# Sigmoid gates of a hybrid attention layer by seven block products instead of eight, on one Trainium2 core

## The chip, the core and the metric

The kernel runs on one core of one Trainium2 chip, as one launch. TensorE (PE) multiplies matrices into PSUM, VectorE (DVE), ScalarE (ACT) and GpSimd (POOL) work element by element, and SyncE (SP) issues every DMA of this kernel in one queue. The metric is the device time of one execution in microseconds (us); lower is better.

## The reference

One layer of an encoder, batch 1, 1024 tokens, width 1024, all in float32 (cut to what matters):

```python
h = rms_norm(x, g_norm1) * (1.0 + sc1) + sh1
qa, ka, va, qb, kb, vb, gates = split(h @ w_in)
o_a = neighbourhood_attention(norm(qa), norm(ka), va, rpb)        # 8 heads of 64
o_b = mixture_of_dilated_windows(rot(qb), rot(kb), vb)            # 3 x 4 heads of 64
gate_a, gate_b = split(sigmoid(gates + b_gate), 2)                # 1024 columns each
merged = gate_a * (o_a @ w_proj_a) + gate_b * (o_b @ w_proj_b)
x = x + gt1 * (merged @ w_o)
h2 = rms_norm(x, g_norm2) * (1.0 + sc2) + sh2
a, up = split(h2 @ w_ffn_in)                                      # 2816 columns each
x = x + gt2 * ((silu(a) * up) @ w_ffn_out)
```

The change concerns `gates = h @ w_g`, a product of 1024 × 1024 by 1024 × 2048.

## The kernel before

Every float32 matrix product is done as three passes: each operand is split into a rounded part `hi` and a rest `lo`, and the products hi·hi, hi·lo and lo·hi are summed in PSUM (`PASS`). So a product over one tile of 128 input rows is three matmuls. A weight comes as `wload` (a DMA into a `raw` tile of 128×512, six such tiles) and is split by `wsplit` (L108, L109): ScalarE copies it to `whi`, and POOL or VectorE subtracts to `wlo`.

The program is a sequence of stages. Up to about 60 us it makes h, transposed and split, in two tiles `hT` (128 × 8 × 1024 each, hi and lo). Then comes a loop over turns n = 6 to 91 (60 to 628 us), one turn after the other: projections of ten units of attention heads (L293), and with them scores (L442), score maxima on VectorE (L456), transposes (L468) and products with v (L483) of items that are spread over three turns; each turn issues the scores of one item, the transposes of the item of the turn before, and the products of the one before that. A turn of the dilated heads is about 6.15 us long. The last turns, n = 80 to 90, have no projection any more, and half products of the gates fill them (`gate_pre`, L602): 24 matmuls each, with 128 gate columns as weights and 512 tokens as moving data. Two such half products share one weight. Their sums wait in DRAM (`sig_d`).

After the loop come, each starting where TensorE's queue reaches it: the gate stage (`gates`, L580 by `mm_set`), which makes the other 21 half products for i = 2 to 7 (i counts blocks of 128 columns in each of the two gates); the merge (again L580, and L877 to L881), the output projection (L1027), the first FFN matrix (L1091) and the second (L1247).

Both FFN matrices are already done with seven block products in place of eight (Winograd's form of Strassen's scheme, one level): the tokens are two blocks, the inner dimension is two blocks, and a pair of outputs is two blocks. The weight blocks w11, w12 and w22 are used plain, and four combinations x1 to x4 are made from differences; the token blocks are mixed in the same manner (`t_columns`). For the second FFN matrix the weight combinations were made by `w2_combos` (L901 to L908) during the gate stage: four loads of 256 KB, two subtractions each on POOL and VectorE, four stores to `w2_d`, eleven times. `w1_combos` does the like for two blocks of the first FFN matrix.

What sets the order: TensorE's instructions stand in program order, by hand. On the other engines a scheduler orders what the code issues. Each engine then works its queue strictly in order; an instruction that has to wait holds all behind it. SyncE waits in the same way before it issues a DMA.

The tiles that matter: `raw` (6), `whi`/`wlo` (10 each), `l` (22, the landing tiles of `w2_combos`, on the right side of SBUF, beside the ten `sg` tiles of the gates), and the attention's own pool on the right side, which is released after the last turn.

Of the kernel before, what the change touches and what calls it, by code (L numbers as in the profile page):

```python
# [27 lines left out]
LATE = (3, 4, 5, 6, 7)  # L28
# [4 lines left out]
NLAND = 22  # L33
W2C = {0: (0,), 1: (1,), 2: (2, 3), 3: (4,), 4: (5,), 5: (6, 7), 6: (8,), 7: (9,), 8: (10,)}
# [9 lines left out]
def hybrid_layer(ctx: ExitStack, tc: tile.TileContext, x, colp, wada1, wada2, bada2, wqkv, wg, wpa, wpb,  # L44
# [16 lines left out]
    sig_d = tc.dram_tile([4, 2, 128, S], F32, name="sig_d")  # L61
# [522 lines left out]
    NPRE = 11  # L584

    def gate_w(i, br):
        if (i, br) not in gw:
            gw[i, br] = [wslot(wg[i, :, 8 * br + 4 * j:8 * br + 4 * j + 4, :], 512) for j in range(2)]

    def gate_pre(n):  # L590

        i, br, hf = n // 4, (n // 2) % 2, n % 2
        hs = slice(hf * 512, hf * 512 + 512)
        st = {}

        def chunk(k):
            if k == 0:
                gate_w(i, br)
                st["p"] = bank("d")
            j, kk = divmod(k, 4)  # L600
            for q, (a, b) in enumerate(PASS):
                nc.tensor.matmul(st["p"], gw[i, br][j][a][:, kk * 128:(kk + 1) * 128], hT[b][:, k, hs],  # L602
                                 start=(k == 0 and q == 0), stop=(k == 7 and q == 2))
            if k == 7:
                if hf == 0:
                    gsig[i, br] = big("gsig")
                dst = gsig[i, br][:, hs]
                nc.scalar.activation(dst, st["p"], AF.Identity, bias=bg_c[:, 8 * br + i:8 * br + i + 1])
                nc.sync.dma_start(sig_d[i, br][:, hs], dst)

        return [lambda k=k: chunk(k) for k in range(8)]

    gw, gsig = {}, {}
# [145 lines left out]
    for n in range(6, 92):  # L759
# [6 lines left out]
        elif n - 80 < NPRE:  # L766
            chunks = gate_pre(n - 80)
        else:
            chunks = []
# [57 lines left out]
    for br in range(2):  # L827
        gate_w(3, br)
    ap_.release()

    sgp = pool("sig", "right")
    sig = {}

    def sig_tile(i, br):
        z = sgp.tile(wide, F32, tag="sg", bufs=10, name="sg")
        for hf in range(2):
            sig.setdefault((i, br, hf), z[:, hf * 512:hf * 512 + 512])

    for i in LATE:
        for br in range(2):  # L840
            sig_tile(i, br)
    sig[2, 1, 1] = sgp.tile([128, 512], F32, name="s2")
    lnd = pool("land", "right")

    def gates(i, br):
        gate_w(i, br)
        for hf in range(2):
            hs = slice(hf * 512, hf * 512 + 512)
            if i * 4 + br * 2 + hf < NPRE:
                continue  # L850
            pb = bank("ds"[br])
            for j in range(2):
                mm_set(pb, gw[i, br][j], hT, 4 * j, 4, 8, 4 * j, hs)
            nc.scalar.activation(sig[i, br, hf], pb, AF.Sigmoid, bias=bg_c[:, 8 * br + i:8 * br + i + 1])

    def sig_load(i, br, hf):
        if i * 4 + br * 2 + hf < NPRE:
            hs = slice(hf * 512, hf * 512 + 512)
            nc.sync.dma_start(sig[i, br, hf], sig_d[i, br][:, hs])
            nc.scalar.activation(sig[i, br, hf], sig[i, br, hf], AF.Sigmoid)  # L860
# [7 lines left out]
    def merge(i):  # L868
        merge_w(i)
        wa, wb = mw[i]  # L870
        for hf in range(2):
            hs = slice(hf * 512, hf * 512 + 512)
            ppa, ppb = bank("tv"[hf]), bank("ds"[hf])
            mm_set(ppa, wa, oT, 0, 4, 4, 0, hs)
            mm_set(ppb, wb, oT, 4, 2, 2, 0, hs)
# [7 lines left out]
    def o_split():  # L883
        for pr in (4, 5, 0, 1, 2, 3):
            for hf in range(2):
# [519 lines left out]
```

## Time and profile before

| | us |
|---|---|
| median of 3 runs | 1546.47 |
| lowest, highest | 1545.89, 1547.77 |
| the profiled execution | 1547.32 |
| its span | 1545.5 |
| attention's turns n = 6 to 91 | 60 to 628.2 |
| gate stage | 628.2 to 742.7 |
| merge | 742.7 to 810.2 |
| output projection | 810.2 to 904.4 |
| first FFN matrix | 904.4 to about 1331 |
| second FFN matrix | about 1331 to the end |

The span is the time from the first to the last instruction that the profile records; the rest of the execution lies around it. The stage bounds are read from the chain of waits, where the line and the PSUM bank of TensorE's instructions change. The granted TensorE clock was 0.999 of full speed.

### The profile page before, as it was taken

Reading aid. Unit: us, or ns where it says so; the run is one execution under the profiler, and the core shown is the slowest. Engines: PE = TensorE matmul, PEld = TensorE weight load, DVE = VectorE, ACT = ScalarE, POOL = GpSimd, SP = SyncE. Lnnn points to the kernel's source line nnn. Section 1 sums busy time; section 2 is a strip of 40 time slices with the busy share of each in tenths; the row PEclk is TensorE's granted clock in tenths of the full one; section 3 lists DMA queues with packets and bytes.
Section 4 is the critical chain, followed back from the end, with each engine's and each line's share of the span. In section 5 each row is a group of like instructions: output and inputs, shape, how many; then the busy total and the mean of one; then the engine's idle time right before and its main releaser. Section 6 shows DMA issues by size and latency. Waiting matters only on the chain.

```text
span 1545.5 us, 24656 instructions
## 1 busy us (share of the span) xinstructions
PE 1523.5 (99%) x8216; PEld 1280.4 (83%) x8216; DVE 1009.0 (65%) x2230; ACT 652.5 (42%) x1702; POOL 635.5 (41%) x618
## 2 busy tenths in 40 slices
PE   9999999999999999999999999999999999999998
PEld 7988888898888877888888888888888888888887
DVE  6776676776889843333475488678867776434477
ACT  5564555555545453224342254223322233344433
POOL 0422331221000031565352220577777777545555
PEclk9999999999999999999999999999999999999999
DMA  9323231443344252896445234344543334576765
GB/s 364 125 85 98 62 117 44 129 132 112 89 132 144 90 174 71 276 382 234 133 136 200 82 109 141 122 153 156 171 135 104 107 105 133 197 217 197 246 216 199
DMA packets 153950, 236.42 MB, mean 153 GB/s; under 512 B 27856, under 2 KB 65616, under 8 KB 153824
## 3 DMA queue, kind: packets, MB, share of 16 engines
q1 hardware_dynamic: 153824, 234.85, 47.1%
q8 instruction: 65, 1.06, 0.3%
q14 instruction: 61, 0.50, 0.1%
HBM read 175.95 MB, written 58.83 MB: 152 GB/s over the span
## 4 chain that ended last, share of the span: by engine, by line
PE 88%; DVE 4%; DMA 3%; issue 2%; ACT 2%; POOL 0%; SPq 0%; DVEq 0%; POOLq 0%; ACTq 0%
PE ps_d L293 14%; PE ps_v L1091 7%; PE ps_d L1091 7%; PE ps_s L1091 7%; PE ps_t L1091 6%; PE ps_s L580 5%; PE ps_d L580 4%; PE ps_d L602 4%; PE ps_d L1247 4%; PE ps_s L1247 4%; PE ps_v L1247 3%; PE ps_t L1247 3%; PE ps_v L483 2%; PE ps_s L442 2%; PE ps_d L1027 2%; PE ps_s L1027 2%
## 5 line engine op out<-in xcount | busy, mean ns | idle before, releaser
L109 POOL TENSOR_TENSOR wlo<-raw,whi 128x512 fp32r<-128x512 f32 (+2 forms) x214 | 281.6, 1323 | 483.5 <-ACT whi L108 403.0
L108 ACT ACTIVATE whi<-raw 128x512 fp32r<-128x512 f32 (+1 forms) x382 | 222.0, 601 | 272.6 <-PE ps_s L1247 42.4
L293 PE MATMUL ps_d<-whi,hT 128*128 128x384 f32 x1152 | 317.8, 344 | 1.3 <-ACT v L328 1.3
L109 DVE TENSOR_TENSOR wlo<-raw,whi 128x512 fp32r<-128x512 f32 (+1 forms) x168 | 155.7, 938 | 100.2 <-ACT whi L108 88.3
L293 PEld LDWEIGHTS ps_d<-whi,hT 128*128 128x128 f32 x1152 | 211.1, 189 | 7.0 <-ACT vs L331 3.5
L293 PE MATMUL ps_d<-wlo,hT 128*128 128x384 f32 x576 | 194.0, 337 | 0.0
L293 PEld LDWEIGHTS ps_d<-wlo,hT 128*128 128x128 f32 x576 | 108.9, 189 | 0.2 <-POOL wlo L109 0.2
L1041 POOL TENSOR_TENSOR e<-e,c 128x512 f32<-128x512 f32 x44 | 67.8, 1541 | 47.9 <-DVE c L1171 25.0
L108 ACT ACTIVATE whi<-ws 128x512 fp32r<-128x512 f32 x60 | 37.8, 630 | 116.3 <-DVE ws L1108 55.0
L323 POOL TENSOR_TENSOR ra<-qn,rtab 128x64 f32<-128x64 f32 x48 | 16.4, 342 | 167.2 <-DVE qn L316 125.5
L457 ACT ACTIVATE P<-P,st 128x256 f32<-128x256 f32 (+2 forms) x100 | 46.2, 463 | 69.5 <-DVE st L456 69.4
L314 DVE TENSOR_REDUCE ss<-sq 128x4 f32<-128x256 f32 x80 | 33.3, 416 | 47.4 <-ACT sq L311 47.3
L1091 PE MATMUL ps_v<-h2T,whi 128*128 128x512 f32 x192 | 59.3, 390 | 0.0
L1091 PE MATMUL ps_s<-h2T,whi 128*128 128x512 f32 x192 | 59.2, 390 | 0.0
L483 PE MATMUL ps_v<-PT,v 128*64 128x128 f32 (+1 forms) x672 | 55.0, 284 | 2.1 <-DVE PT L472 2.1
L1091 PE MATMUL ps_d<-h2T,whi 128*128 128x512 f32 x184 | 56.9, 390 | 0.0
L1039 ACT ACTIVATE e<-e 128x512 f32<-128x512 f32 x44 | 27.4, 630 | 69.2 <-DVE e L1174 47.3
L457 ACT ACTIVATE P<-P,sx 128x384 f32<-128x384 f32 (+1 forms) x64 | 37.1, 580 | 46.3 <-DVE sx L456 46.3
L468 PE MATMUL ps_t<-ident,P 128*128 128x128 f32 (+1 forms) x336 | 51.7, 275 | 4.0 <-DVE P L460 1.7
L442 PE MATMUL ps_s<-qk 64*128 64x256 f32 (+3 forms) x492 | 53.8, 321 | 1.8 <-DVE st L456 1.2
L602 PE MATMUL ps_d<-hT,whi 128*128 128x512 f32 x176 | 55.4, 396 | 0.0
L442 PEld LDWEIGHTS ps_s<-qk 64*128 64x128 f32 (+1 forms) x492 | 35.0, 182 | 23.7 <-issue 11.5
(369 smaller groups left out, 3913.9 us busy)
## 6 DMA issues: line engine op xcount, KB each, us to landing
raw<-in_w_dram SPq DMA_DIRECT2D x139, 256.0 KB
ga_d<-e SPq DMA_DIRECT2D x77, 256.0 KB
raw<-ga_d SPq DMA_DIRECT2D x77, 256.0 KB
wa<-in_wada_dram SPq DMA_DIRECT2D x32, 512.0 KB
raw<-in_wqkv_dram SPq DMA_DIRECT2D x80, 192.0 KB
l<-in_w_dram SPq DMA_DIRECT2D x52, 256.0 KB
w_d<-l SPq DMA_DIRECT2D x52, 256.0 KB
raw<-w_d SPq DMA_DIRECT2D x52, 256.0 KB
```

The source lines that it names most:

```text
L108: nc.scalar.activation(hi[:, :n], r, AF.Copy)
L109: (eng or nc.gpsimd).tensor_sub(lo[:, :n], r, fview(hi[:, :n]))
L293: nc.tensor.matmul(pd[:, :384], tok(a, k, t), U.w[k][b][:, :384], start=(k == 0 and i == 0), stop=(k == KT - 1 and i == 2))
L442: nc.tensor.matmul(I.pS[h][:nq, :nk], U.qk[a][hs, I.q0:I.q0 + nq], U.qk[2 + b][hs, I.kb0 * 128:I.kb0 * 128 + nk], start=(i == 0), stop=(i ...
L457: nc.scalar.activation(P[:nq, :nk], P[:nq, :nk], AF.Exp, scale=-1.0, bias=nm, accum_out=sm)
L483: nc.tensor.matmul(po[hs, :nq], U.v[:, I.kb0 + i, hs], I.PT[h][:, i, :nq], start=(i == 0), stop=(i == nkb - 1))
L580: nc.tensor.matmul(pb, wsl[a][:, j * 128:(j + 1) * 128], src[b][:, ksrc + j, hs], start=(done == 0 and j == 0 and i == 0), stop=(done + j ...
L602: nc.tensor.matmul(st["p"], gw[i, br][j][a][:, kk * 128:(kk + 1) * 128], hT[b][:, k, hs], start=(k == 0 and q == 0), stop=(k == 7 and q == 2))
L1027: nc.tensor.matmul(pbs[hf], h2T[a][:, k, t * 128:(t + 1) * 128], wow[hf, k][b], start=(n == 0 and (a, b) == PASS[0]), stop=(n == KT - 1 an ...
L1041: nc.gpsimd.tensor_mul(sg, sg, up)
L1091: nc.tensor.matmul(pb, w[p][:, k * 128:(k + 1) * 128], b[q][:, k], start=(k == 0 and i == 0), stop=(k == 3 and i == 2))
L1247: nc.tensor.matmul(pb[m], o[0][a][:, m * 128:(m + 1) * 128], o[1][b], start=(k == 0 and i == 0), stop=(k == HT - 1 and i == 2))
```

## The change

The gates are now computed for each i as a 2 × 2 block product with seven products of 12 matmuls, 512 tokens each. The two gates' columns i are the two output blocks. The token blocks are: h's block (0,0) for w11, (1,0) for w12 and (1,1) for x4, plain, and four mixed ones for x1, x2, x3 and w22.

- `t_piece`, called in every second turn from n = 14 by the code, makes the mixed blocks: 16 times four sums of hi and lo, four differences, four ScalarE copies and four rests of 128×128, then one store of 512 KB to DRAM (`t_d`).
- `gate_early` fills turns 80 to 90 with the products w11 and w12 of all eight i and x4 of the first six; two of 12 matmuls per turn, where one of 24 stood. Sums go to `sig_d` and `p3_d`.
- In turn 80 the mixed block of x1 is loaded over h's block (0,1), which is no longer read.
- After the loop six loads of 1 MB bring the blocks of x2, x3 and w22 (`tg`), into the memory that attention's pool has left.
- `gate_mixes` makes the combinations x1, x2, x3 (and x4 for i = 6, 7) of the gate weights on VectorE, which also splits them; `gate_prod` and `gate_end` do the remaining 34 products, the sums of results and the sigmoid. Gates of i = 0 to 2 go to DRAM again until the merge.
- `w2_combos` moves into the first FFN stage, one call after every second block of columns, with its tiles taken from the `c` tiles there (7). `w1_combos` moves to the merge. `o_split`, the split of the attention's result, is done by VectorE alone, into the tiles of the token blocks.

```diff
+GEARLY = tuple((i, nm) for i in range(8) for nm in ("w11", "w12")) + tuple((i, "x4") for i in range(6))
+GORD, GLATE, GAWAY = ("x1", "x2", "x3", "w22"), ("w22", "x3", "x2", "x1", "x4"), 3
+TP0 = 14
...
+    def gate_mm(pb, w, b, k):
+        for q, (x, y) in enumerate(PASS):
+            nc.tensor.matmul(pb, w[x][:, k * 128:(k + 1) * 128], b[y][:, k],
+                             start=(k == 0 and q == 0), stop=(k == 3 and q == 2))
...
+    def t_piece(m):
+        kk, pc = divmod(m, 4)
+        st = big("tp", [128, 8, 128], F32R)
+        y = [fview(st[:, 2 * i + 1, :]) for i in range(4)]
+        y11, y22, y12, y21 = y
+        for z, (k, c) in zip(y, ((0, 0), (1, 1), (0, 1), (1, 0))):
+            cs = slice(512 * c + 128 * pc, 512 * c + 128 * pc + 128)
+            nc.vector.tensor_add(z, *(fview(h[:, 4 * k + kk, cs]) for h in hT))
+        nc.vector.tensor_sub(y11, y12, y11)
+        nc.vector.tensor_sub(y12, y22, y12)
+        nc.vector.tensor_sub(y22, y22, y11)
+        nc.vector.tensor_sub(y21, y21, y22)
+        for i in range(4):
+            nc.scalar.activation(st[:, 2 * i, :], y[i], AF.Copy)
+            nc.vector.tensor_sub(st[:, 2 * i + 1, :], y[i], fview(st[:, 2 * i, :]))
+        nc.sync.dma_start(t_d[:, :, kk, 128 * pc:128 * pc + 128].rearrange("s p c -> p s c"), fview(st))
...
-        elif n - 80 < NPRE:
-            chunks = gate_pre(n - 80)
+        elif n - 80 < len(GEARLY) // 2:
+            chunks = gate_early(n - 80)
...
+        if TP0 <= n < TP0 + 32 and (n - TP0) % 2 == 0:
+            t_piece((n - TP0) // 2)
+        if n >= 79:
+            for z in GEARLY[2 * (n - 79):2 * (n - 78)]:
+                gate_weight(*z)
+        if n == 80:
+            for z, src in zip(hblk(0, 1), (t_d[0], t_d[1])):
+                nc.sync.dma_start(fview(z), src)
...
+    def gate_mixes(i):
+        r = {q: gate_raw(i, q) for q in ((0, 2, 3, 1) if i > 5 else (0, 2, 3))}
+        s1 = wp.tile([128, 512], F32, tag="raw", bufs=NRAW, name="ws")
+        nc.vector.tensor_add(s1, r[2], r[3])
+        nc.vector.tensor_sub(r[2], r[0], r[2])
+        nc.vector.tensor_sub(r[0], r[3], r[2])
+        z = {"x1": s1, "x2": r[0], "x3": r[2], "w22": r[3]}
...
+        for nm in (GLATE if i > 5 else GORD):
+            gwt[i, nm] = wsplit(z[nm], nc.vector)
...
+    for n, nm in enumerate(("x2", "x3", "w22")):
+        for q in range(2):
+            nc.sync.dma_start(fview(tbg[nm][q]), t_d[2 * n + 2 + q])
...
-    GS = [(2, 1)] + [(i, br) for i in LATE for br in range(2)]
-    for n, z in enumerate(GS):
...
-        gates(*z)
-        for k in W2C.get(n, ()):
-            w2_combos(k)
...
+    gate_mixes(1)
+    for i in range(2):
+        gate_begin(i)
+    for n, nm in enumerate(GORD):
+        if n == 2:
+            gate_mixes(2)
+        for i in range(2):
+            gate_prod(i, nm)
...
+    for i in range(2, 6):
+        gate_begin(i)
+        gate_mixes(i + 1)
+        for nm in GORD:
+            gate_prod(i, nm)
+        gate_end(i)
+    gate_mixes(7)
...
+    for nm in GLATE:
+        for i in (6, 7):
+            gate_prod(i, nm)
+    oT = {}
+    o_split()
...
         pair_out(j)
+        if n % 2:
+            w2_combos(n // 2)
```

The order that the scheduler makes of it shows at three places. First SyncE's queue around turns 79 to 81, before (`o_d` and `v_d` are stores of attention results and of v, `v<-v_d` loads v back, `sig_d` stores gate sums, `raw<-in_wg_dram` loads a block of a gate weight):

```order
L487 DMA o_d<-stg 128x128
L333 DMA v_d<-vs 128x128
L344 DMA v<-v_d 128x1x128 x8
L487 DMA o_d<-stg 128x128
L609 DMA sig_d<-gsig 128x512
L101 DMA raw<-in_wg_dram 128x512
L264 DMA mod_d<-row 1x512
L101 DMA raw<-in_wg_dram 128x512 x5
```

and after, with `hT<-t_d` the two loads of 1 MB of the mixed block for x1, each of which waits for TensorE's last read of the old block:

```order
L866 DMA hT_107<-t_d 128x4x512
L866 DMA hT_392<-t_d 128x4x512
L489 DMA o_d<-stg 128x128
L335 DMA v_d<-vs 128x128
L346 DMA v<-v_d 128x1x128 x8
L489 DMA o_d<-stg 128x128
L625 DMA sig_d<-gsum 128x1024
L103 DMA raw<-in_wg_dram 128x512
L266 DMA mod_d<-row 1x512
L103 DMA raw<-in_wg_dram 128x512 x11
```

The two loads stand ahead of the last v store, and the first weight block behind the v loads is now one that turn 81 uses (w11 of i = 1); before, that load brought a weight of turn 82.

Second, SyncE's queue where the loop ends and the gate stage begins, before (`l<-in_w_dram` are the loads of `w2_combos`):

```order
L487 DMA o_d<-stg 128x128
L609 DMA sig_d<-gsig 128x512
L487 DMA o_d<-stg 128x128
L901 DMA l<-in_w_dram 128x512 x9
L908 DMA w_d<-l 128x512
```

and after (`p_d` holds the sums of x4, `tg` are the token blocks, `sg` the gate sums):

```order
L631 DMA p_d<-gsum 128x512
L489 DMA o_d<-stg 128x128
L103 DMA raw<-in_wg_dram 128x512
L898 DMA tg<-t_d 128x2048 x6
L908 DMA sg<-sig_d 128x1024 x3
L103 DMA raw<-in_wg_dram 128x512
L103 DMA raw<-p_d 128x512
```

The six loads stand behind the last store of an attention result, and the loads of gate sums behind them.

Third, VectorE's queue near turn 10, before (`qk` is the normalized q or k, `acc` sums the conditioning vector, `P,st` the score maximum):

```order
L371 SCALAR_TENSOR_TENSOR qk<-ps_s,hg,qk 128x128
L372 TENSOR_TENSOR qk<-ps_s,qk 128x128
L122 TENSOR_TENSOR rz<-ry,rv 128x4
L123 SCALAR_TENSOR_TENSOR rz<-rz,ry 128x4
L124 SCALAR_TENSOR_TENSOR ry<-rz,ry 128x4
L282 SCALAR_TENSOR_TENSOR acc_1085<-wa_1230,cact,acc_1085 128x512 x2
L456 ISA P,st<-ps_s,bmask 64x128
```

and after (`tp` are tiles of `t_piece`):

```order
L643 TENSOR_TENSOR tp<-hT_107,hT_392 128x128 x6
L373 SCALAR_TENSOR_TENSOR qk<-ps_s,hg,qk 128x128
L374 TENSOR_TENSOR qk<-ps_s,qk 128x128
L124 TENSOR_TENSOR rz<-ry,rv 128x4
L644 TENSOR_TENSOR tp<-tp 128x128
L284 SCALAR_TENSOR_TENSOR acc_1087<-wa_1232,cact,acc_1087 128x512
L644 TENSOR_TENSOR tp<-tp 128x128
L125 SCALAR_TENSOR_TENSOR rz<-rz,ry 128x4
L645 TENSOR_TENSOR tp<-tp 128x128
L458 ISA P,st<-ps_s,bmask 64x128
```

The pieces' operations stand between those of the attention, ahead of the score maximum; the scheduler takes them four turns earlier than the code issues them, and in bursts of three to five pieces.

More of the change, by code (lines that the diff above doesn't have):

```diff
@@ L582, in mm_set @@
                                  stop=(done + j == ntot - 1 and i == 2))
[L584 to L596, printed above, removed]
-            if k == 0:
[L598 to L611, printed above, removed]
```

172 lines of the change are left out of this document (122 added, 50 removed).

## The prediction

> **What bounds the kernel now.** I read the page first: busy shares, granted clock, the chain that ended last.
>
> ```profile
> span 1545.5 us, 24656 instructions
> PE 1523.5 (99%) x8216; PEld 1280.4 (83%) x8216; DVE 1009.0 (65%) x2230; ACT 652.5 (42%) x1702; POOL 635.5 (41%) x618
> ...
> PE 88%; DVE 4%; DMA 3%; issue 2%; ACT 2%; POOL 0%; SPq 0%; DVEq 0%; POOLq 0%; ACTq 0%
> ```
>
> TensorE works 99% of the span, so the time is matmul time plus few waits. The view of TensorE's waits begins with
>
> ```profile
> PE ps_v L483 <- DVE PT L472: 2.1, 3, 1.0
> PE ps_t L560 <- ACT PT L474: 1.7, 1, 1.7
> ```
>
> and all its lines together stay under 20 us. Two things follow: a matmul removed in a stage where TensorE never waits is its full duration gained, and any new wait of TensorE is paid in full. The profiled execution took 1547.32 us (span 1545.5, about 1.8 around it), 0.85 above the median, 1546.47. I sum against 1547.32 and take 0.85 off at the end.
>
> From the chain of waits, which here is TensorE's own order (start, duration, what), the places that the change touches:
>
> ```profile
> 542.37 2.76 PE ps_d L602 x12
> ...
> 551.40 2.95 PE ps_d L602 x12
> ...
> 556.73 5.47 PE ps_d L602 x24
> ...
> 627.63 0.59 PE ps_v L483 x8
> 628.22 5.71 PE ps_s L580 x24
> 633.92 10.88 PE ps_d L580 x48
> ...
> 742.72 2.81 PE ps_t L580 x12
> ...
> 974.27 2.81 PE ps_v L1091 x12
> 977.08 2.73 PE ps_d L1091 x12
> ```
>
> Gate products are fitted into attention from 542.37 (turn n = 80); the gate stage proper runs without a gap from 628.22 to the merge at 742.72, 114.5 us. A 512-column matmul costs 10.88/48 = 0.2267 us. A product of 12 takes 2.73 us on blocks of h and 2.81 us on the FFN's t tiles (L1091, second-last row).
>
> **Part 1: fewer products.** Before, 32 half products of 24 matmuls, 768. After, 8 times 7 block products of 12, 672. In attention stand 11 × 24 = 264 before and 22 × 12 = 264 after, in the same turns. The gate stage goes from 504 to 408: 96 × 0.2267 = 21.8 us less. Of its 34 products 24 (x2, x3, w22) read t tiles on SBUF's right side; if they cost what the FFN's do, 24 × (2.81 − 2.73) = 1.9 us come back. **−19.9 us**, 94.6 instead of 114.5.
>
> **Part 2: the weight of turn 81.** SyncE's queue from the timeline, and the first gate load's landing from the chain:
>
> ```profile
> 500.31 3.62 DMA raw<-in_wg_dram
> 543.26 0.32 SPq L333 DMA_DIRECT2D v_d<-vs  x1
> 546.16 4.94 SPq L344 DMA_DIRECT2D v<-v_d  x8
> 551.21 0.40 SPq L487 DMA_DIRECT2D o_d<-stg  x1
> 551.70 0.38 SPq L609 DMA_DIRECT2D sig_d<-gsig  x1
> 552.13 0.42 SPq L101 DMA_DIRECT2D raw<-in_wg_dram  x1
> ...
> 628.79 0.39 SPq L487 DMA_DIRECT2D o_d<-stg  x1
> 629.27 4.31 SPq L901 DMA_DIRECT2D l<-in_w_dram  x9
> ```
>
> ```profile
> L108 ACT ACTIVATE whi<-raw 128x512 fp32r<-128x512 f32 x294 | 179.7, 627 | 265.8 <-PE ps_s L1247 42.4 <-PE ps_t L1247 28.8 <-PE ps_d L1091 26.6
> L109 POOL TENSOR_TENSOR wlo<-raw,whi 128x512 fp32r<-128x512 f32 x161 | 228.8, 1426 | 315.7 <-ACT whi L108 236.0 <-DMA raw<-in_wg_dram 51.8 <-PE ps_t L468 18.3
> ```
>
> ```profile
> 628.00:685.00 57.00, 57.00 (x255) 47.04 (x252) 21.95 (x19) 14.41 (x22) 37.80 (x28) 1.00 0.99 358
> 685.00:743.00 58.00, 58.00 (x257) 48.04 (x256) 16.43 (x14) 22.33 (x35) 33.67 (x25) 1.00 0.73 257
> 585.00:628.00 43.00, 43.00 (x276) 33.90 (x272) 14.28 (x52) 15.36 (x38) 7.73 (x6) 1.00 0.27 78
> 150.00:175.00 25.00, 25.00 (x180) 22.78 (x179) 18.08 (x60) 14.93 (x55) 9.38 (x21) 1.00 0.41 135
> 971.00:1331.00 360.00, 360.00 (x1563) 293.35 (x1562) 264.76 (x298) 108.09 (x182) 254.63 (x178) 1.00 0.40 128
> ```
>
> (Groups: busy us, mean ns of one, idle before. Windows: length; busy us of PE, PEld, DVE, ACT, POOL; clock; DMA share; GB/s.)
>
> Before, turns 80 and 81 share one weight, so the load at 552.13 serves turn 82 and is early. After, each turn takes two new weights, and turn 81's w11 is this same load, still behind the eight v loads. They wait for the v store of 543.26 to land, and SyncE issues in order, so o_d, sig_d and the weight wait with them. Even with nothing else in the way it is issued at about 552.1, lands 3.62 later at 555.8, and is copied and subtracted (ACT 0.6, POOL 1.4) by 557.8. TensorE wants it at 551.40: 6.4 us. But two loads of 1 MB (h's block 01, mixed) now stand ahead of the v store; they go once TensorE has left the old block, at 542.37. With the queue saturated it moves 358 GB/s, so 2.1 MB take 5.9 us; a 256 KB load took 3.62 where 0.73 is transfer, so 2.9 is fixed. They land near 542.4 + 2.9 + 5.9 = 551.2, and if the v store lands no earlier, everything behind it moves by 551.2 − 546.2 = 5.0 us. So 6.4 to 11.4; I take **+11**, since packets of one queue share the engines in order. In-order TensorE has nothing to put in between.
>
> **Part 3: token blocks at the start of the gates.** Six 1 MB loads (x2, x3, w22) fill tiles of attention's released memory, and stand on SyncE behind the last o_d store (628.79), so x2's 2 MB land at about 629.2 + 2.9 + 5.9 = 638.0. TensorE has only x1 of i = 0 and 1, two products of 2.73, until 628.2 + 5.5 = 633.7: 4.3 us idle. Then 2 MB every 5.9 us against pairs of 5.6 us adds 0.6. **+5** (2, if the loads go out two us earlier or the hi half starts the product, to 12, if the sig loads or the other traffic interleave).
>
> By the Trainium skill's page "SBUF — State Buffer", section "The DMA setup-cost knee", a transfer costs about 2 us plus its bytes at 436 GB/s. By that rule 2 MB would take 6.8 us instead of 8.8, and parts 2 and 3 together would give about 12 instead of 16, the sum landing within 0.2% of before. The 358 GB/s of the saturated window speaks against the rate, so I keep the rows.
>
> **Part 4: making the blocks.** Sixteen pieces (t_piece), each 12 VectorE operations of 128×128, 4 ScalarE copies and one store. The start-to-start time of such an operation is seen at
>
> ```profile
> 87.99 0.28 DVE L372 TENSOR_TENSOR qk<-ps_v,qk 128x128 fp32r<-128x128 f32 x1
> 88.18 0.15 DVE L124 SCALAR_TENSOR_TENSOR ry<-rz,ry 128x4 f32<-128x4 f32 x1
> ```
>
> 0.19 to 0.28, about 2.6 us a piece, 42 us in all. The order puts them in bursts of 5, 4, 4, 3 over four turns or so (n near 10, 21, 29, 42), ahead of VectorE's score maximum that TensorE's transposes two turns later rest on. In 150–175 (four turns of 6.15) VectorE is busy 18.1 of 25 and has 6.9 free. Bursts of 13, 10.4, 10.4, 7.8 us overrun it by 6, 3.5, 3.5 and 1: 14 us if nothing absorbed it. About a turn of slack (the scores run ahead of their products) lies before each burst, which would absorb all. Between 0 and 14 I take **+5**, nearer to the cover, as the pieces lie directly ahead of the maxima in the order.
>
> **Part 5: mixed weights.** In turns 80–90 VectorE makes x4 for six gates: 28 more loads of 256 KB, and three subtractions each, on 14.3 of 43 us used and DMA share 0.27: hidden but for a late load, **+0.5** (0 to 3). In the gate stage it has, per gate, some 13 operations of 0.69 (L1070 below), 9 of 11.2 us; o_split moves fully to VectorE, under the four products (11 us) that follow x2 of gate 7, and w1_combos to the merge: **+0.5** (0 to 4). What ran there before goes away: the window 628–685 shows DMA at 0.99 and POOL 37.8 of 57 with TensorE at 57.00, so removing that gains nothing.
>
> **Part 6: w2_combos in the FFN.** Per k two POOL and two DVE subtractions, 4 loads and 4 stores.
>
> ```profile
> L903 POOL TENSOR_TENSOR l<-l 128x512 f32<-128x512 f32 x11 | 15.6, 1415 | 0.6 <-DMA l<-in_w_dram 0.5
> L904 DVE TENSOR_TENSOR l<-l 128x512 f32<-128x512 f32 x11 | 9.7, 882 | 24.9 <-DMA l<-in_w_dram 18.5 <-POOL l L903 6.4
> L905 POOL TENSOR_TENSOR l<-l 128x512 f32<-128x512 f32 x11 | 14.2, 1288 | 9.6 <-DVE l L904 9.6
> L906 DVE TENSOR_TENSOR l<-l 128x512 f32<-128x512 f32 x11 | 15.1, 1372 | 18.5 <-POOL l L905 14.7 <-DMA l<-in_w_dram 2.4 <-DMA w_d<-l 1.4
> L1070 DVE TENSOR_TENSOR c<-h2T,h2T 128x512 f32<-128x512 f32 x16 | 10.6, 694 | 0.0
> ```
>
> That is 15.6 + 14.2 = 30 us more POOL and 9.7 + 15.1 = 25 more DVE, in a window where POOL has 254.6 of 360 and DVE 264.8: 79% and 80% after. TensorE never waits there now, and 22 MB over 360 us are 63 GB/s beside 128. In-order waits for a c load (up to 3.6 us, eleven times) are mostly eaten by the weights made ahead: **+1.5** (0 to 12).
>
> **Sum:** −19.9 + 11 + 5 + 5 + 0.5 + 0.5 + 1.5 = +3.6: 1547.3 + 3.6 = 1550.9 profiled, **1550** beside the median.
>
> **The rivals.**
> A, the forecast: two DMA waits and some VectorE delay eat the gain. 1550. Own range 1544 to 1556; chance 0.40.
> B, the change pays: the v store is not delayed and the pieces are covered, so 6.4 + 2 to 5 + 1 remain of the costs. 1546.5 − 19.9 + 6.4 + 3 + 1 = 1537 (1530 if even turn 81's load came early, for which it would have to be issued before 551.40 − 2.0 − 3.62 = 545.8; the row at 546.16 speaks against it). For it: small DMA shares and VectorE's free quarter. 0.32.
> C, POOL and DVE become the bound of the FFN pairs, ending on the slow side: L906 took 1372 ns beside POOL where L1070 took 694, so mixing stretches both engines. If each of the 11 pairs of columns lost 1 us more, 1550 + 11 = 1561. It decides from the point where either engine passes its share of about 28 us per two columns; at 80% it does not on average. 0.12.
> The Trainium skill's page "SBUF — State Buffer", section "Who interferes with whom", has it that a VectorE tensor_tensor with both inputs in SBUF and a GpSimd operation that reads SBUF exclude each other for the whole instruction. L906 agrees with it. By that rule the mixing would add to the sum of both engines' times (265 + 255 + 55 in 360), and C would be likely. That so many of these run beside each other now without one TensorE wait keeps its chance low.
> D, the piece bursts are not absorbed and spread to ScalarE's copies: 14 instead of 5, with 12 in part 3: 1550 + 16 = 1566. 0.12.
> E, the change does not do what it says: the mixing costs so many waits in the gate stage itself that its 114.5 us stay, 1550 + 15 = 1565. For it, VectorE's 9 of 11.2 us per gate; against it, eight banks of results in flight. 0.04.
>
> **How the numbers follow.** The range takes in B's 1537 and reaches into C and D up to 1563, leaving out the 1530 end of B and the rest of D. Within 0.2% of 1546.5 (±3.1 us, about what a measurement here can tell from no change) lies the lower part of A and the upper of B. Faster: most of B, 0.30. Same: 0.22. Slower: the rest of A, C, D, 0.48.
>
> **What would show it.** Right: the gate stage from first product to merge near 94.6 + 5; a TensorE wait near 551 of about 11 us released by the split of w11; one of 4 us after the second gate product; the pieces' turns slightly longer than 6.15. Wrong: no wait at 551 (B), TensorE waits in 971–1331 (C), waits for score maxima before n = 45 above 10 us (D). My forecast fails first if packets of the v store pass the 2 MB, or if the weight of turn 81 is there in time.

## The result, and the profile after

The changed kernel takes 1631.86 us (median of 4, 1631.24 to 1636.89) beside 1546.18 for the kernel before: a ratio of 1.0561, 95% interval 1.0538 to 1.0584. The profiled execution took 1636.89, the longest of the four, 5 us over their median. The page's head and shares, and TensorE's clock:

```profile
span 1635.1 us, 25136 instructions
PE 1540.4 (94%) x8120; PEld 1284.2 (79%) x8120; DVE 1160.0 (71%) x2564; ACT 678.7 (42%) x1787; POOL 629.7 (39%) x602
```

```profile
core 0: 1635.1 us, clock 0.975
```

The 96 matmuls are gone (8216 to 8120), and still the span is 89.6 us longer. Span less PE's busy time is 94.7 us now, 22.0 before: 72.7 us of new idle time. PE's busy time has grown by 16.9 although 96 × 0.2267 = 21.8 us of it left, so about 38.7 us went into the matmuls that stayed. Most of that is the clock: it stood at half for 81.9 us in all, in 14 stretches. For 63.3 us of them TensorE was busy, and half of that, 31.7 us, is what it would have saved at full clock; before, it was 1.5. The other 8.5 us of longer matmuls are not placed further. So 72.7 + 38.7 − 21.8 = 89.6.

Where it stands, by the starts of the stages on TensorE (the third version is the best one of the experiments, third_mend; the starts before are read from the chain of waits, the others from the timeline, which has such a start up to 0.2 us earlier):

| us from the span's start | before | after | third_mend |
|---|---|---|---|
| turn 80, first gate product | 542.4 | 572.25 | 542.47 |
| end of attention | 628.2 | 679.5 | 639.1 |
| merge | 742.7 | 782.8 | 734.9 |
| output projection | 810.2 | 850.3 | 802.4 |
| first FFN matrix | 904.4 | 951.9 | 898.9 |
| second FFN matrix | 1331.2 | 1412.1 | 1336.5 |
| end of span | 1545.5 | 1635.1 | 1554.7 |

Before to after: attention up to turn 80 +29.9, turns 80 to 91 +21.4, gate stage −11.2, merge 0, output projection +7.4, first FFN matrix +33.4, second +8.7. Of the +29.9 some 3 to 6 us belong to this one execution: w11_early, w2_ahead, gates_of_three and fill_the_wait below, which run the same code up to turn 78 at least, reach turn 80 at 566.1 to 569.6. The waits that stand there, from the view of TensorE's waits (bank and line, what released it, total us, times, longest):

```profile
PE ps_v L353 <- POOL qn L328: 18.8, 6, 6.0
PE ps_d L605 <- ACT whi L110: 7.8, 1, 7.8
PE ps_d L1207 <- DVE e L1280: 6.6, 2, 4.3
PE ps_d L1143 <- DVE sg L982: 5.6, 1, 5.6
PE ps_s L605 <- DMA tg<-t_d: 5.4, 2, 3.4
PE ps_v L1207 <- DVE e L1290: 4.5, 2, 3.1
```

Before, the longest single wait of this view was 1.7 us. The first row is the pieces in attention, the second turn 81's weight, the third and last the FFN, the fourth the output projection, the fifth the token blocks. A long one costs more than it shows, as the windows around the first burst tell (length; busy us of PE, PEld, DVE, ACT, POOL; granted clock, DMA share, GB/s):

```profile
96.00:102.02 6.02, 0.01 (x2) 0.01 (x1) 5.46 (x29) 3.47 (x14) 3.32 (x5) 0.77 0.66 208
99.29:106.12 6.83, 4.10 (x15) 4.11 (x16) 4.91 (x23) 2.26 (x9) 3.62 (x7) 0.50 0.57 178
106.20:116.00 9.80, 9.19 (x62) 8.24 (x61) 5.78 (x27) 5.33 (x22) 1.06 (x4) 1.00 0.32 95
```

TensorE does nothing for 6.0 us; from 99.29 the clock is half, for 6.83 us, of which 4.1 are matmuls after the wait has ended, and only then full again. What VectorE did meanwhile, from its timeline (start, us, line, operation):

```profile
96.24 0.16 DVE L122 TENSOR_SCALAR rv<-ss 128x4 f32<-128x4 f32 x1
96.31 0.69 DVE L643 TENSOR_TENSOR tp<-hT,hT 128x128 f32<-128x128 f32 x3
...
97.65 0.28 DVE L643 TENSOR_TENSOR tp<-hT,hT 128x128 f32<-128x128 f32 x1
97.85 0.16 DVE L124 TENSOR_TENSOR rz<-ry,rv 128x4 f32<-128x4 f32 x1
97.92 0.28 DVE L644 TENSOR_TENSOR tp<-tp 128x128 f32<-128x128 f32 x1
98.12 0.42 DVE L318 TENSOR_TENSOR qn<-qn,ry 128x256 f32<-128x256 f32 x1
...
100.44 0.41 DVE L318 TENSOR_TENSOR qn<-qn,ry 128x256 f32<-128x256 f32 x1
```

The steps that normalize q and k (rv, rz, ry, qn) are a chain of small operations, and between them stand piece operations (`tp`). POOL's rotation of q and k (L325 to L328) waits for qn, and TensorE's transposes of it (L353) wait for L328. The rotation itself was slow here too. One of its operations while VectorE worked at the pieces, and the same one behind them:

```profile
99.85 1.71 POOL L327 TENSOR_TENSOR rb<-qn,rtab 128x32 f32<-128x32 f32 x1
102.41 0.25 POOL L327 TENSOR_TENSOR rb<-qn,rtab 128x32 f32<-128x32 f32 x1
```

With L326 (0.99 us, else 0.25) that is 2.2 of the 6.0 us; no run shows the one without the other.

In the FFN, the timelines of SyncE, POOL and VectorE (in brackets the idle time before a row, and what ended it):

```profile
1114.53 1.85 SPq L1007 DMA_DIRECT2D c<-in_w_dram  x4
```

```profile
1120.73 1.29 POOL L1009 TENSOR_TENSOR c<-c 128x512 f32<-128x512 f32 x1 [5.45 <-DMA c<-in_w_dram]
```

```profile
1122.06 1.76 DVE L1010 TENSOR_TENSOR c<-c 128x512 f32<-128x512 f32 x1 [6.14 <-POOL c L1009]
1123.74 1.74 DVE L1223 TENSOR_TENSOR ws<-raw 128x512 f32<-128x512 f32 x1
1125.40 0.68 DVE L1290 TENSOR_TENSOR e<-e,ps_v 128x512 f32<-128x512 f32 x1
```

```profile
1126.23 0.47 PE L1207 MATMUL ps_v<-h2T,whi 128*128 128x512 f32 x1 [3.06 <-DVE e L1290]
```

The loads go out at 1114.5; POOL's first subtraction waits 5.45 us for them, VectorE's waits 6.14 us for POOL, and the sum that would free TensorE's bank (L1290) stands behind it in the queue. TensorE loses 3.06 us there, and 1.7 more at the half clock behind it (3.41 us).

### The profile page after: what moved, and what is told of

Its sections match the earlier page's. It is cut to its first block, busy times and chain, and to the rows that moved or that the text cites. A ratio compares the mean times of both kernels' runs of the same rounds, so it can differ in the third digit from the quotient of the medians.

```text
span 1635.1 us, 25136 instructions
## 1 busy us (share of the span) xinstructions
PE 1540.4 (94%) x8120; PEld 1284.2 (79%) x8120; DVE 1160.0 (71%) x2564; ACT 678.7 (42%) x1787; POOL 629.7 (39%) x602
## 5 line engine op out<-in xcount | busy, mean ns | idle before, releaser
L111 POOL TENSOR_TENSOR wlo<-raw,whi 128x512 fp32r<-128x512 f32 (+2 forms) x204 | 270.8, 1337 | 564.5 <-ACT whi L110 533.9
L295 PE MATMUL ps_d<-whi,hT 128*128 128x384 f32 x1152 | 323.8, 350 | 1.4 <-ACT v L330 1.4
L110 ACT ACTIVATE whi<-raw 128x512 fp32r<-128x512 f32 (+2 forms) x398 | 230.5, 601 | 227.2 <-PE ps_s L1365 35.2
L111 DVE TENSOR_TENSOR wlo<-raw,whi 128x512 fp32r<-128x512 f32 (+1 forms) x194 | 179.2, 937 | 104.1 <-ACT whi L110 93.9
L295 PEld LDWEIGHTS ps_d<-whi,hT 128*128 128x128 f32 x1152 | 216.6, 193 | 7.0 <-ACT vs L333 3.5
L295 PE MATMUL ps_d<-wlo,hT 128*128 128x384 f32 x576 | 197.4, 343 | 0.0
L110 ACT ACTIVATE whi<-ws 128x512 fp32r<-128x512 f32 x68 | 42.6, 626 | 123.4 <-DVE ws L1224 86.4
L325 POOL TENSOR_TENSOR ra<-qn,rtab 128x64 f32<-128x64 f32 x48 | 17.3, 360 | 188.2 <-DVE qn L318 145.1
L1157 POOL TENSOR_TENSOR e<-e,c 128x512 f32<-128x512 f32 x44 | 71.3, 1620 | 26.7 <-DVE e L1156 13.7
L605 PE MATMUL ps_d<-hT,whi 128*128 128x512 f32 x192 | 63.6, 414 | 11.1 <-ACT whi L110 7.8
L1156 DVE TENSOR_TENSOR e<-e 128x512 f32<-128x512 f32 x44 | 51.6, 1172 | 15.0 <-ACT e L1155 15.0
```

Of the source, the lines that this page charges most:

```text
L110: nc.scalar.activation(hi[:, :n], r, AF.Copy)
L111: (eng or nc.gpsimd).tensor_sub(lo[:, :n], r, fview(hi[:, :n]))
L295: nc.tensor.matmul(pd[:, :384], tok(a, k, t), U.w[k][b][:, :384], start=(k == 0 and i == 0), stop=(k == KT - 1 and i == 2))
L605: nc.tensor.matmul(pb, w[x][:, k * 128:(k + 1) * 128], b[y][:, k], start=(k == 0 and q == 0), stop=(k == 3 and q == 2))
L1156: nc.vector.tensor_mul(sg, sg, a)
L1157: nc.gpsimd.tensor_mul(sg, sg, up)
```

## The experiments

The theory after this comparison: each part waits at one place for something that stands late in an in-order queue, and TensorE's idle time is then paid a second time by the clock. The rival: the work added (VectorE 1009 to 1160 us busy, and 22 MB moved into the FFN) is itself too much for the engines or the DMA. If the theory holds, the same work in another order costs little.

### pieces_pinned

`t_piece` is issued behind the turn's transposes, and its sums can't be taken earlier by the scheduler.

```diff
-            nc.vector.tensor_add(z, *(fview(h[:, 4 * k + kk, cs]) for h in hT))
+            tc.keep_in_program_order(nc.vector.tensor_add(z, *(fview(h[:, 4 * k + kk, cs]) for h in hT)))
```

> The changed kernel, with each t_piece held behind the transposes of its own turn on VectorE: one piece every second turn instead of bursts of five, four, four and three. The work is the same. Theory (bursts): the 30 us by which projections run late at turn 80 (572.2 against 542.2) come only from the bursts, which delay q and k for TensorE by more than its slack and make it idle, and each idle of some 2 us or more also halves TensorE's clock for several us. Spread, 2.6 us a piece fits into VectorE's 3.4 us free in two turns: projections reach turn 80 at 543 to 548, the whole at about 1605. Rival (too much work): the 42 us of VectorE do not fit, however they are spread: turn 80 at 560 or later, the whole at 1620 or more.

1610.74 us, ratio 1.0430 [1.0400, 1.0460]. Turn 80 starts at 550.89, 8.7 us late instead of 29.9. The bursts are most of the loss in attention; what is left arises at three places (3.9, 3.5 and 2.9 us).

### w11_early

Gate weights one turn earlier; the two 1 MB loads over h's block wait until turn 85.

```diff
-        if n >= 79:
-            for z in GEARLY[2 * (n - 79):2 * (n - 78)]:
+        if n >= 78:
+            for z in GEARLY[2 * (n - 78):2 * (n - 77)]:
...
-        if n == 80:
+        if n == 85:
```

> The changed kernel, with the gate weights of each turn from 80 on loaded one turn earlier, and the two 1 MB loads of x1's token block held back to turn 85. Theory (weight wait): the wait of 7.8 us at 581 and the 10.2 us at half clock behind it (5.1 lost) go, 13 us less, 1619; the turns 80 to 90 keep the smaller waits for the gates' sums on VectorE (about 5 us). Rival (shift): what is late next in these turns (VectorE's mixing for x4, or the loads) takes the place of most of it: less than 5 us won.

1616.3 us, 1.0466 [1.0436, 1.0497]. The 7.8 us wait is gone, and the half clock after it; turns 80 to 91 take 94.3 us instead of 107.2. They are still about 8.4 us over before, so this wait was not all that these turns lost. (Its profiled execution is also 5.5 us earlier at turn 80, by the scatter named above.)

### w2_ahead

The loads of `w2_combos` are issued one block of columns ahead of its subtractions.

```diff
+        if n % 2:
+            w2_load(n // 2)
...
-        nc.gpsimd.tensor_sub(t1, b[0, 1], b[0, 0])
+        tc.keep_in_program_order(nc.gpsimd.tensor_sub(t1, b[0, 1], b[0, 0]))
```

> The changed kernel, with w2_combos split: its four loads are issued before the second column block of a pair, and the mixing stands behind that block's last GpSimd operation; eight c tiles instead of seven. Arithmetic and traffic are the same. Theory (in-order waits): GpSimd's and VectorE's first mixing operations wait for loads just issued (24.6 and 29.4 us in the pairs) and hold up the sums of products behind them; with the loads ahead the 33 us that the first FFN matrix grew fall to under 10, the whole to 1600 to 1610. Rival (load on the engines): POOL and VectorE with 55 us more work in 375 are the bound; the FFN stays above 450 us and the whole above 1622.

1603.71 us, 1.0385 [1.0323, 1.0446]. The first FFN matrix takes 437.3 us (460.2 after, 426.8 before), the second 218.7 (223.0, 214.3): the same loads, stores and subtractions, with one more `c` tile (8), 28 us cheaper.

### before_w2_in_ffn

The kernel before, with `w2_combos` alone moved into the FFN, by the changed kernel's own code.

```diff
-W2C = {0: (0,), 1: (1,), 2: (2, 3), 3: (4,), 4: (5,), 5: (6, 7), 6: (8,), 7: (9,), 8: (10,)}
+W2C = {8: ()}
...
+        if n % 2:
+            w2_combos(n // 2)
```

> The kernel before, with nothing changed but the place of w2_combos: out of the gate stage, into the first FFN matrix as in the change. Theory (own price): this part alone costs what the first FFN matrix and the start of the second lose in the changed kernel, 33 + 9 us: 1585 to 1590, TensorE's waits in the pairs with clock losses behind them. Rival (brought along): these stages are late in the changed kernel because of what comes before (the merge's late end, w1_combos, the sums), and the part alone costs under 15 us: below 1562.

1584.16 us, 1.0258 [1.0228, 1.0288]: 40 us for this part alone, with the same waits of TensorE on FFN sums (6.7 and 4.5 us at the head of the view). It needs nothing else of the change.

### gates_of_three

The first three gates run together, so that more products stand ahead of the token blocks' loads, and `w1_combos` comes earlier in the merge.

```diff
-        if n in (2, 5):
-            w1_combos(n // 3, EARLY[n // 3])
+        if n in (0, 2):
+            w1_combos(n // 2, EARLY[n // 2])
```

> The changed kernel with two edits at the two ends of the gate stage: the first three gates go together (three x1 products of 8.2 us in all, before the first product on a loaded block, instead of two of 5.5), and w1_combos runs behind the first and third merge instead of the third and sixth. Theory (loads behind the last store): the two waits for token blocks (3.4 and 2.0 us, and 3.4 us of clock) shrink to about 2 in all; the wait of 5.6 us at the start of the output projection (and its 3.4 us of clock) came from w1_combos' loads in VectorE's queue and goes: 1631.9 - 6 - 9 = about 1617. Rival: the token blocks are late by the traffic, and the third x1 only moves the wait behind it; and the projection waits for the merge's last sums anyway: 1628 to 1632.

1619.44 us, 1.0478 [1.0447, 1.0510]. The waits for `tg` are gone, and the gate stage takes 95.5 us (103.3 after). The output projection's wait is halved, 2.79 instead of 5.62; over all runs it is 3.9 to 7.5 us where `w1_combos` was left in its place and 1.5 to 3.2 where it was moved. What is left has another cause: on ScalarE two copies of the next weights wait 2.06 and 1.25 us for their loads, and the copy of the merge's result (L984) stands behind them. (Here the profiled execution is 6.2 us earlier at turn 80, where nothing was changed.)

### all_mended

The four edits together, the pieces in chosen turns (12, 14, 18, 20, 22 and so on).

> All mends in one: pieces pinned, in turns that are not the first or the last two of a unit (12 to 52); gate weights a turn earlier; w2_combos loaded ahead; the first three gates together; w1_combos early in the merge. The seven products and all added work stay. Theory (the loss is waits with their clock, not the work): 1546 less 20 for the products, plus about 3 left of the pieces, 5 in turns 80 to 90, 2 at the token blocks, 12 of the pairs' share and the second FFN's start: 1548, within 1540 to 1556. Rival (the added work itself does not fit, and each mend moves its wait elsewhere): above 1570.

1581.62 us, 1.0229 [1.0206, 1.0253]: missed, because two of the mends moved the wait. Turn 80 is still 21 us late: a piece in the seventh turn of a unit collides with the weight splits of the next turn on VectorE, 4.4 to 7.5 us at turns 17, 25, 33, 49. And turns 80 to 91 take 98.4 us, as ScalarE's timeline shows:

```profile
589.48 0.63 ACT L110 ACTIVATE whi<-raw 128x512 fp32r<-128x512 f32 x1 [3.66 <-DMA raw<-in_wg_dram]
590.01 0.58 ACT L622 ACTIVATE gsum<-ps_d 128x512 f32<-128x512 f32 x1
```

The copy of a weight waits 3.66 us for its load, and the copy that empties TensorE's bank (L622) stands behind it.

### w2_in_attention

All of that, with `w2_combos` in turns 48 to 78 of attention, on POOL alone, in place of the FFN.

> As all_mended, but w2_combos goes out of the FFN into attention's turns 48 to 78, one call every third turn, all four subtractions on GpSimd (which is busy 5 of 40 us there), tiles from attention's ring of seven. Theory (the pairs have no room, these turns have): the FFN stages are as before the change, 427 and 209 us, and the time is that of all_mended less 10 to 14: about 1535, below before. Rival (attention pays): the ring or the queue on SyncE holds up the loads of v and of the bias tables there, as the pieces did: attention's turns 48 to 79 get 10 us or more longer, and the time is 1545 or above.

1625.39 us, 1.0508 [1.0484, 1.0532]. The FFN is as before the change (427.1 us), but attention pays more than was won:

```profile
PE ps_d L605 <- ACT gsum L622: 15.6, 1, 15.6
PE ps_t L470 <- DVE oacc L570: 13.7, 1, 13.7
```

A spare engine is no spare place: the loads and stores stand in SyncE's one queue, ahead of attention's own, and between 440 and 660 us SyncE waited 32.8 us for POOL's subtractions before it could issue their stores.

### second_mend

The pieces in the second, fourth and sixth turn of a unit; gate loads two turns ahead and their copies pinned late; four calls of `w2_combos` among the FFN's early products, seven later.

```diff
-TPN = (12, 14, 18, 20, 22, 26, 28, 30, 34, 36, 38, 42, 44, 46, 50, 52)
+TPN = (12, 17, 19, 21, 25, 27, 29, 33, 35, 37, 41, 43, 45, 49, 51, 53)
```

> all_mended with three places changed by its trace. Pieces in the second, fourth and sixth turn of a unit, never in the seventh and eighth, whose weight splits already fill VectorE (its losses of 4 to 7 us stood at turns 17, 25, 33, 49, each behind a piece in a seventh turn). Gate weights: loads two turns ahead, ScalarE's copies only behind the turn before their use (a copy that waited 3.7 us for its load held up a gate sum there), and the two 1 MB loads apart, in turns 82 and 84. w2_combos: four of eleven calls among the early products of the FFN, on GpSimd alone, the others every third block instead of every second. Theory (waits in order): attention reaches turn 80 within 6 us of before (21 late in all_mended), turns 80 to 91 within 4 (12), the FFN stages within 8 (15): 1581.6 - 15 - 8 - 7 = about 1552. Rival (no room for the added work): the waits turn up at other turns and the time stays above 1570.

1587.06 us, 1.0290 [1.0263, 1.0316]: the first edit works (turn 80 at 544.4, 2 us late), the other two fail. Pinned copies make TensorE wait 12.2 us in all for `whi` in turns 80 to 91, and the early FFN has a new wait of 6.79 us. So only the first was kept.

### fill_the_wait

The changed kernel, with 32 matmuls of 512 columns into an unused bank ahead of turn 81's first product. They change no result; they keep TensorE busy while it waits.

```diff
+                if (i, nm) == (1, "w11"):
+                    z = bank("d")
+                    for _ in range(32):
+                        nc.tensor.matmul(z, gwt[0, "w12"][0][:, :128], hblk(0, 0)[0][:, 0], start=True, stop=True)
```

> The changed kernel, with 32 matmuls of 512 columns (7.3 us, results not used) put before the first product of turn 81, where TensorE waits 7.8 us for its weight. Theory (the clock is halved by the idle): TensorE works through the wait, so the half-clock stretch of some 10 us behind it (5.1 us lost) does not come, while the product starts when it did: from turn 80 to the gate stage 102 us instead of 107, and no record of half clock between 580 and 600. Rival (the clock falls for another reason, as by a switch of load): the stretch stays, and the time is as in the changed kernel or up to 7 us longer.

1624.15 us, 1.0515 [1.0494, 1.0536]. The windows of the wait and of what follows, after the change:

```profile
580.00:600.00 20.00, 12.04 (x56) 8.09 (x55) 3.42 (x9) 8.12 (x18) 10.72 (x9) 0.74 0.69 216
589.00:600.00 11.00, 10.60 (x51) 7.94 (x52) 2.05 (x7) 7.69 (x18) 10.72 (x9) 0.76 0.69 214
```

and with the filling:

```profile
575.00:583.90 8.90, 8.88 (x36) 6.04 (x35) 1.36 (x2) 0.59 (x1) 0.00 (x0) 1.00 0.71 226
583.90:600.00 16.10, 15.31 (x94) 11.76 (x95) 6.93 (x20) 11.49 (x27) 15.99 (x13) 1.00 0.72 223
```

The weight comes as late (16.8 us behind the start of turn 80, 17.0 without the filling), the loads are as busy, and the clock stays at 1.00: here the idle time halves it, not the load. It won little time: turn 80 to the end of attention is only 1.6 us shorter (105.7). The stretch that it saved held 4.8 us of TensorE's work, so only 2.4 us of loss, and TensorE, now faster, waited 2.08 and 2.06 us later on, each with a half-clock stretch of 3.41 us. The rest of the 7.7 us is not the filling's: the profiled execution reaches turn 80 at 567.2 instead of 572.25 and has a first FFN matrix 5.2 us shorter, where the two kernels don't differ.

### pieces_placed

The changed kernel, only with the pieces as in second_mend.

> The changed kernel with the pieces alone moved, as in second_mend: pinned, one in the second, fourth and sixth turn of each unit (12 to 53); everything else as in the change. Theory (placement is all of the pieces' price): turn 80 within 2 us of the kernel before (30 late in the changed one, 8.7 with one piece every second turn), the whole 1631.9 - 29 = about 1603. Rival (the pieces' price moves into later turns or comes back with the other edits absent): turn 80 over 8 us late, the whole above 1610.

1600.99 us, 1.0362 [1.0341, 1.0383]. TensorE's timeline has the first gate product at

```profile
543.61 0.39 PE L605 MATMUL ps_d<-hT,whi 128*128 128x512 f32 x1
```

1.2 us late instead of 29.9. All sixteen pieces are still made, with the same operations. Their place in VectorE's queue was nearly the whole price.

### third_mend

pieces_placed, w11_early, w2_ahead and gates_of_three together.

> all_mended with the pieces of second_mend, and nothing else of it: gate weights a turn earlier, w2_combos loaded ahead in every second block of the pairs, first three gates together, w1_combos early. Theory (the prices add up by place): all_mended's 1581.6 less the 20 us that its pieces still cost: 1560 to 1563, which is slower than before by what is left: 12 in turns 80 to 91, 5 in the output projection, 15 in the FFN, against 19 won in the gates. Rival (an earlier end of attention only makes another wait longer): above 1570.

1557.74 us, 1.0098 [1.0071, 1.0125], the best version that computes the same result, and still about 1% slower than before. The clock is 0.995. The gate stage takes 734.9 − 639.1 = 95.8 us, 18.7 less than before. That is spent again: turns 80 to 91 +10.9, output projection +2.3, the FFN +10.8 and +3.9.

### traffic_only

third_mend without the four subtractions of `w2_combos`; its loads and stores stay, and the second FFN matrix is multiplied with the plain blocks.

> third_mend without the four subtractions of w2_combos: its 44 loads and 44 stores stay, so the second FFN matrix is multiplied with unmixed blocks in four of its seven products. Theory (the arithmetic, 28 us on GpSimd and 28 on VectorE in queues that are three quarters full): the 10.7 us that the first FFN matrix is still longer than before fall to under 3, the second FFN's 3.8 to under 2, the whole to about 1546. Rival (the traffic: 23 MB more, and stores and loads in SyncE's queue ahead of the weights): the first FFN stays above 434 us and the whole above 1553.

1542.38 us, 0.9987 [0.9971, 1.0002]. The FFN's windows of four kernels (columns as above), before the change in the fifth row of the prediction's windows, then after, third_mend and traffic_only:

```profile
1037.00:1412.00 375.00, 353.55 (x1484) 284.36 (x1483) 287.32 (x298) 97.35 (x175) 281.72 (x189) 0.97 0.51 171
```

```profile
984.00:1336.00 352.00, 345.06 (x1481) 279.55 (x1480) 279.98 (x298) 97.33 (x173) 276.06 (x188) 0.99 0.56 181
```

```profile
984.00:1326.00 342.00, 342.00 (x1484) 278.79 (x1483) 256.64 (x286) 101.42 (x175) 246.84 (x171) 1.00 0.58 192
```

Some 1480 matmuls take 375, 352 and 342 us. With 192 GB/s moved, traffic_only has TensorE at 342.00 of 342: the traffic is hidden. The 23 us between the first two are a matter of order, gone by loading ahead; the 10 us between the last two go with the 44 subtractions, their engine time and what they wait for, and remain in third_mend.

## Why the prediction was wrong

1550 was forecast, up to 1563; 1632 was measured. The sign was the likelier one, the size was not in the range.

Two steps failed by far the most: part 6 (+1.5 forecast, 42 measured) and part 4 (+5 forecast, 24 to 30 measured). Behind both, and behind the other waits, the premise was short of a term.

**The premise.** "Any new wait of TensorE is paid in full" leaves out the clock: a wait cost its length and, where the clock then fell, another 1.6 to 3.0 us, which is half of TensorE's work in the stretch at half clock. With 72.7 us of new idle time that came to some 30 us. The prediction had the granted clock in each window it quoted (1.00) and never asked what an idle TensorE does to it.

**Part 1** (−19.9) was right: −18.7 in third_mend, where the token blocks are in time.

**Part 2** (+11) named the load, the queue and the wait. Measured were 7.8 us of wait, and 2.4 of clock: the stretch of 10.24 us began during the wait, and only 4.8 us of TensorE's work fell into it. The sum of 10.2 is near the forecast by luck, as SyncE's timeline shows:

```profile
567.67 1.20 SPq L866 DMA_DIRECT2D hT<-t_d  x2
...
573.30 0.33 SPq L335 DMA_DIRECT2D v_d<-vs  x1
577.49 4.95 SPq L346 DMA_DIRECT2D v<-v_d  x8
...
583.47 0.42 SPq L103 DMA_DIRECT2D raw<-in_wg_dram  x1
```

The two big loads go out 4.6 us before turn 80 (572.25), not at its start, so the v store is delayed less: 4.2 us from its issue to the v loads, 2.9 before (543.26 to 546.16). The weight was issued 11.2 us after turn 80's start, where the prediction's own terms give 14.8. It landed 5.1 us after its issue, not 3.62, and the first product waited only for the copy to `whi`, 0.7 us, not for both halves of the split (2.0). That makes 7.8 of the 11.4 us; the clock, which the prediction did not have, made up for most of the difference.

The other 11 us of the +21.4 in turns 80 to 91 were not foreseen: 6.6 us of further waits and 3.0 of clock, the rest not placed. The longest wait, of 2.31 us, on VectorE and TensorE:

```profile
620.17 1.36 DVE L596 TENSOR_TENSOR raw<-raw 128x512 f32<-128x512 f32 x1 [1.64 <-DMA raw<-in_wg_dram]
621.45 0.41 DVE L462 TENSOR_SCALAR P<-P,sx 128x384 f32<-128x384 f32 x1
621.78 0.15 DVE L461 RECIPROCAL sx<-sx 128x1 f32<-128x1 f32 x1
```

```profile
622.01 1.80 PE L470 MATMUL ps_t<-ident,P 128*128 128x128 f32 x6 [2.31 <-DVE sx L461]
```

L596 is the mixing of x4, and it waits for its load at the head of VectorE's queue; the scaling of the scores (L461, L462), for which TensorE's transposes wait, stands behind it. The next longest, 1.73 us, is a gate sum (L624) behind two mixing operations of the gate stage's weights.

**Part 3** (+5): waits of 3.43 and 2.00 us, 5.4 in all, and 2.7 of clock. The size without the clock was right.

**Part 4** (+5, 0 to 14) was +29.9 here, 24 to 27 in the four other runs of the same code. The bursts, their turns and their 42 us of VectorE were as told. Two steps were not: "about a turn of slack lies before each burst" holds for the score maxima, while the chain that normalizes q and k, a few small operations one behind the other, has no such slack; and the bound of 14 summed overrun, though a chain is delayed by every foreign operation between its links (6.0 us for the burst's worst wait, the slowed rotation included). Rival D had the mechanism, on the wrong chain and at half the price. pieces_placed shows that placing alone settles it.

**Part 5**: "hidden but for a late load" was wrong by such loads, each at the head of VectorE's queue. In turns 80 to 91 it is the wait of L596 above. In the merge `w1_combos` waits 2.44 us for its load (at 828.4), and at the start of the output projection TensorE waits 5.62 us for the merge's last sums, with 1.9 of clock; gates_of_three, which moves `w1_combos`, shows about half of that wait to be its doing.

**Part 6** (+1.5, 0 to 12) failed worst: the mixing costs 33.4 + 8.7 us here and 40 in before_w2_in_ffn. The step that failed is "mostly eaten by the weights made ahead". The waits were put at 3.6 us; they were up to 7.0, and behind them stood, besides weights, the sums that empty TensorE's banks. Rival C, VectorE or POOL as the bound, is not what happened: they are busy 287 and 282 of 375 us, 77% and 75%. The row of L1010 above has 1.76 us, while POOL is busy with a split (L111, 1121.98 to 1123.27); L1012, the same kind of operation, takes 0.68 us at 1129.37, begun while POOL is idle. That is as the Trainium skill's page "SBUF — State Buffer", section "Who interferes with whom", has it, the rule weighed in the prediction. It may be a share of the 10 us which traffic_only leaves to the arithmetic; how much of it was not tried.

**What stays open** is the 10.9 us that third_mend still loses in turns 80 to 91; it has waits of up to 1.4 us there, 5.9 in all, and a half-clock stretch of 6.83 (3.0 us lost), and no run took them away.

## What to carry to other kernels

Where TensorE is busy 99% of the time, an edit is priced by the longest new wait at the head of each in-order queue it touches, not by busy shares: here the same work cost 24 to 30 us or 1.2 (the pieces), and 42 or 15 (the second matrix), by its place alone. Issue a load well ahead of the operation that reads it, keep bulk work out of queues in which a chain of small dependent operations runs, and look at which operation empties TensorE's banks behind it. And count a wait of about 2 us or more with the half clock that can follow it.

## What the runs showed of the clock

That the clock halves after so short an idle time was not expected. In third_mend's timeline TensorE waits once for over 2 us in attention:

```profile
169.56 0.69 PE L353 MATMUL ps_v<-ident,qn 128*128 128x128 f32 x2 [2.25 <-POOL qn L328]
```

and the windows around it and around two shorter waits close together (1.41 us, and the start of one of 1.05) have

```profile
166.01:169.42 3.41, 1.30 (x15) 0.83 (x14) 3.41 (x10) 1.96 (x7) 3.41 (x6) 1.00 0.34 96
169.42:172.83 3.41, 3.27 (x13) 3.28 (x14) 1.48 (x6) 1.33 (x4) 1.28 (x6) 0.50 0.32 101
606.33:609.74 3.41, 1.68 (x18) 1.05 (x14) 1.85 (x6) 0.00 (x0) 0.00 (x0) 1.00 0.87 266
609.74:613.15 3.41, 2.68 (x6) 2.15 (x7) 2.49 (x5) 1.31 (x3) 1.27 (x1) 0.50 0.65 198
```

2.25 us of idle time, then 3.41 us at half speed. Over all kept traces the stretches were 3.41 or 6.83 us long, four times 10.24 and once each 13.65 and 23.89, at 0.50. In each trace they begin on one grid of 3.413 us (after the change at 99.29, then 22, 39 and 142 steps later at 174.38, 232.41 and 583.98), which the waits do not set. Cut along this grid from 12 us on, the fourteen traces show what decides: a window at full clock with TensorE busy for less than 47% of it was followed by one at half in 103 of 104 cases, one busy for more than 61% in none of 6079, and between the two in 13 of 85. From half the clock came back behind a window that was at least 82% busy (116 of 118), never behind one under 80% (68). So the length of a wait alone does not tell. After the change an idle time of 2.08 us at 87.65 had no stretch, because the grid cuts it in two:

```profile
85.64:89.05 3.41, 2.01 (x15) 1.39 (x13) 3.41 (x12) 1.97 (x9) 2.15 (x3) 1.00 0.33 114
89.05:92.46 3.41, 2.73 (x16) 2.49 (x17) 3.41 (x17) 1.82 (x8) 0.55 (x2) 1.00 0.42 124
```

The Trainium skill's page "TensorE: Matmul & The Clock Gate", section "What's actually happening", gives two states, full and half, and a free-running window of about 3.4 us after whose idling the clock halves. The two states, the grain of 3.41 us and the free running agree. Its section "HAM oscillation — how this bites in real kernels" puts the rule as no idle gaps over about 3.4 us; here 2.25 us was enough, and so were two short gaps close together, so the measurement decides: about half of a window idle does it, and gaps of 2 us are to be avoided as well.
